# Two products instead of three in the feature-major GEMMs of a bidirectional SSD layer, with a new division of PSUM

## The chip, the core and the metric

The kernel runs on one core of one Trainium2 chip. The metric is the device time in microseconds of one execution, as a median of several. The data are float32; products are made in `float32r` on operands that are split into a high and a low part, so that the result has nearly float32 precision.

## What is computed

One layer on 256 tokens of 2048 features: a bidirectional Mamba-2 mixer (SSD), a cross-attention with 4 heads into 256 memory tokens, and a gated FFN with a convolution, each ahead of a residual add, and a last RMSNorm. Cut to what matters:

```python
u = rmsnorm(h, mix_norm)
z, xbc, dt_raw = split(u @ w_in)                       # 4096, 4096 + 2*8*128, 128
xs, B, C = split(silu(dwconv(xbc, conv_w, conv_b)))    # 64 heads of 64; 8 groups of state 128
y = ssd_scan(xs, dt_f, A_f, B, C) + flip(ssd_scan(flip(xs), ...)) + xs * d_skip
h = h + rmsnorm(y * silu(z), norm_g) @ w_out           # chunks of 128 tokens inside ssd_scan
u, mem_n = rmsnorm(h, xattn_norm), rmsnorm(mem, mem_norm)
q, (k, v) = u @ wq, split(mem_n @ wkv)
h = h + softmax(q k^T * 512**-0.5) v @ wo
gate, val = split(rmsnorm(h, ffn_norm) @ w_up)         # 5632 each
h = h + (silu(dwconv(gate)) * val) @ w_down
out = rmsnorm(h, final_norm)
```

## The kernel before

**Operands in two parts.** An activation operand is held in units (`new_unit`, line 94) of four feature tiles of 128 by 256 tokens, high and low part side by side, from a pool of 11. Weights come by DMA on SyncE's queue into `raw` (five buffers, line 115) in pieces of 1024 columns' worth per partition. ScalarE casts a piece to `w_hi` (line 106) and VectorE makes `w_lo` (line 107), four buffers each: 618 pieces in all.

**Three kinds of GEMM.** `gemm_feat` (line 132) puts features on the partitions and makes, for each of the contraction's tiles and each tile of 128 features, three products of 256 columns: high times high, high times low, low times high (lines 152 to 154). A PSUM tile of two banks takes four feature tiles. `gemm_feat_wide` (line 157) makes two: the high part of the weights meets both parts of the operand in one product of 512 columns (line 169), and the low part meets the high part in one of 256 (line 171). A feature tile then has a bank to itself, whose halves ScalarE (line 173) and VectorE (line 174) add up. Only the FFN's up-projection uses it. `gemm_tok` (line 176), for the values and the down-projection, puts tokens on the partitions.

**PSUM.** Eight banks: `ps_g`, two tiles of two banks for GEMMs by feature, and `ps_m`, four of one bank for all else (lines 60 and 61). Both are open from the first to the last instruction.

**Stages.** x is transposed and split; dt, its running sums and decays are made (to line 352). Then eight groups: `project(g+1)` (xs: four feature tiles, B and C: two; convolution and silu), `project_z(g)` (four), and `scan_group(g)` (line 389). The scan transposes xs and B, makes the two states that leave the chunks (line 415), and then for each of two chunks: a DMA broadcasts the running sums into `r` (line 420, one buffer), eight heads pass through ScalarE and VectorE (lines 431 and 432), an exponential (434), eight more passes (437 and 438), a product with it (440), TensorE's products with the incoming state (444) and with xs (449), and the additions (452 to 456). Behind the last group, `inv_rms` (line 223, matmuls 225 and 226, first reader 215) makes 1/rms of y in `r_ssd` (last instruction: line 221). Then come the memory tokens (a pool `memp` of their own, DMA in line 497, transposes in 515), w_out with the residual (`residual_units`, lines 476 and 484), queries, keys, values and attention, wo, and the FFN.

**What sets the order.** The Tile scheduler writes each engine's order: among the instructions that are ready in its own simulation it takes the one that is earliest in the program. It also sets the waits between pools that use the same memory one after the other.

Of the kernel before, what the change touches and what calls it, by code (L numbers as in the profile page):

```python
# [14 lines left out]
P = 128  # L15
T = 256
# [20 lines left out]
def kernel(  # L37
# [22 lines left out]
    ps_g = ctx.enter_context(tc.tile_pool(name="ps_g", bufs=2, space=bass.MemoryType.PSUM))  # L60
    ps_m = ctx.enter_context(tc.tile_pool(name="ps_m", bufs=4, space=bass.MemoryType.PSUM))
# [23 lines left out]
    # tri[:, 0, l] = 1 where l >= m, tri[:, 1, l] = 1 where l <= m  # L85
# [46 lines left out]
    def gemm_feat(units, wv, cols, k_first=0, first_raw=None):  # L132
        """features on the partitions: banks of two 128-feature tiles by 256 tokens"""
# [23 lines left out]
    def gemm_feat_wide(units, wv, c0, dst):  # L157
        """dst [P, 2, T] = two 128-feature tiles; the high part of the weights meets both parts of the
        operand in one product, so each tile has a bank whose halves add up to it"""
        nk = 4 * len(units)  # L160
        ps = psum_g()
        for k0 in range(0, nk, 4):
            hi, lo = load_weights(wv, k0, [(c0, 2 * P)])
            for kk in range(4):
                kt = k0 + kk
                unit = units[kt // 4]
                for ft in range(2):
                    fs = slice(ft * P, (ft + 1) * P)
                    nc.tensor.matmul(ps[:, ft, :], hi[:, kk, fs], unit[2][:, kt % 4].rearrange("p s t -> p (s t)"),  # L169
                                     start=(kt == 0), stop=False, skip_group_check=True)  # L170
                    nc.tensor.matmul(ps[:, ft, :T], lo[:, kk, fs], unit[0][:, kt % 4, :], start=False,  # L171
                                     stop=(kt == nk - 1), skip_group_check=True)
        nc.scalar.copy(out=dst, in_=ps[:, :, T:])
# [27 lines left out]
    def add_square(pool, acc, src2, first):  # L201
        """src2: [P, 2, T]"""
# [7 lines left out]
    def rsqrt_mean(pool, dst, total, n, tags=("rs_v", "rs_s")):  # L210
        """dst = (total / n + eps) ** -0.5: a square root from the table, then one Heron step"""
# [16 lines left out]

    r_mix = sb(const, [P, T], "r_mix")
# [7 lines left out]
    w_in_v = kview(w_in)  # L237
    units_mix = [new_unit() for _ in range(4)]
    with tc.tile_pool(name="xin", bufs=1) as xin:
# [9 lines left out]
        for u in range(4):  # L249
            stage = sb(xin, [P, 4, T], "x_stage", bufs=2)  # L250
            for jj in range(2):
                ps = psum_m()
# [19 lines left out]
        # the column of 1/rms as a row on every partition  # L272
# [12 lines left out]
    with tc.tile_pool(name="ssd", bufs=1) as ssd:  # L285
        acc_y = sb(ssd, [P, 2, T], "acc_y")

# [10 lines left out]
        # log1p(ex) = ln(w) * ex / (w - 1) with w = 1 + ex, and ex itself where w == 1  # L298
# [32 lines left out]
        # decay to the end of the chunk times dt: forward for chunk 0, backward for chunk 1  # L331
# [12 lines left out]
        # exp(cum) where a state comes in: forward rows in chunk 1, backward rows in chunk 0  # L344
# [9 lines left out]
        def conv_silu(banks, f0s, dst):  # L354
            """centred conv of 4 taps over the tokens, bias, silu; two feature tiles per bank"""
            for b, bank in enumerate(banks):
                s = sb(ssd, [P, 2, T], "cv_s", bufs=2)
                nc.vector.tensor_tensor(out=s, in0=two(bank), in1=rows2(r_mix), op=ALU.mult)
                a = dst[:, 2 * b:2 * b + 2, :]
                for j in range(2):  # L360
                    f = f0s[2 * b + j]
                    w = lambda t: pcol("conv_w", f * 4 + t)
                    nc.scalar.activation(out=a[:, j, :], in_=s[:, j, :], func=AF.Identity, scale=w(2), bias=pcol("conv_b", f))
                    for tap, off in ((0, 2), (1, 1)):
                        nc.vector.scalar_tensor_tensor(out=a[:, j, off:], in0=s[:, j, :T - off], scalar=w(tap),
                                                       in1=a[:, j, off:], op0=ALU.mult, op1=ALU.add)
                    nc.vector.scalar_tensor_tensor(out=a[:, j, :T - 1], in0=s[:, j, 1:], scalar=w(3),
                                                   in1=a[:, j, :T - 1], op0=ALU.mult, op1=ALU.add)
                nc.scalar.activation(out=a, in_=a, func=AF.Silu)

        def project(g):
            xs = sb(ssd, [P, 4, T], "xs", bufs=2)
            conv_silu(gemm_feat(units_mix, w_in_v, [(INNER + g * 512, 512)]), [g * 4 + j for j in range(4)], xs)
            bc = sb(ssd, [P, 2, T], "bc", bufs=2)
            conv_silu(gemm_feat(units_mix, w_in_v, [(2 * INNER + g * P, P), (2 * INNER + 1024 + g * P, P)]),
# [3 lines left out]
        def project_z(g):  # L379
            sz = sb(ssd, [P, 4, T], "sz")  # L380
            for b, bank in enumerate(gemm_feat(units_mix, w_in_v, [(g * 512, 512)])):
                nc.vector.tensor_tensor(out=sz[:, 2 * b:2 * b + 2, :], in0=two(bank), in1=rows2(r_mix), op=ALU.mult)
                nc.scalar.activation(out=sz[:, 2 * b:2 * b + 2, :], in_=sz[:, 2 * b:2 * b + 2, :], func=AF.Silu)
# [5 lines left out]
        def scan_group(g, xs, bc, sz):  # L389
            hs = slice(g * 8, (g + 1) * 8)  # L390
            er = sb(ssd, [P, 2, 4, P], "er")
            for q in range(2):
                for d in range(2):
                    nc.sync.dma_start(out=er[q * 64:(q + 1) * 64, d], in_=ecum_v[g, q, d].partition_broadcast(64))
            # token-major x and B
            xs_tok = sb(ssd, [P, 2, 512], "xs_tok")
            xsd = sb(ssd, [P, 2, 512], "xsd")
            for c in range(2):
                ps = psum_m()
                for j in range(4):  # L400
                    nc.tensor.transpose(out=ps[:, j * P:(j + 1) * P], in_=xs[:, j, c * P:(c + 1) * P], identity=ident)  # L401
                nc.scalar.copy(out=xs_tok[:, c, :], in_=ps)
                nc.vector.tensor_tensor(out=xsd[:, c, :].rearrange("p (h f) -> p h f", f=64),
                                        in0=ps.rearrange("p (h f) -> p h f", f=64),
                                        in1=dx_tok[:, c, hs].unsqueeze(2).broadcast_to([P, 8, 64]), op=ALU.mult)
            b_tok = sb(ssd, [P, 2, P], "b_tok")
            ps = psum_m()
            for c in range(2):
                nc.tensor.transpose(out=ps[:, c * P:(c + 1) * P], in_=bc[:, 0, c * P:(c + 1) * P], identity=ident)
            nc.scalar.copy(out=b_tok.rearrange("p c n -> p (c n)"), in_=ps[:, :T])  # L410
            # state that leaves chunk 0 forwards, and the one that leaves chunk 1 backwards
            st = sb(ssd, [P, 2, 512], "st")
            for c in range(2):
                ps = psum_m()
                nc.tensor.matmul(ps, b_tok[:, c, :], xsd[:, c, :], start=True, stop=True)  # L415
                nc.scalar.copy(out=st[:, c, :], in_=ps)
            for c in range(2):
                cl = slice(c * P, (c + 1) * P)
                r = sb(ssd, [P, 2, 8, P], "r")
                nc.sync.dma_start(out=r, in_=cum_v[c, g].partition_broadcast(P))  # L420
                ps_cb = psum_m()
                nc.tensor.matmul(ps_cb[:, :P], bc[:, 0, cl], bc[:, 1, cl], start=True, stop=True)
                cb = sb(ssd, [P, 2, P], "cb")
                nc.vector.tensor_tensor(out=cb, in0=ps_cb[:, :P].unsqueeze(1).broadcast_to([P, 2, P]), in1=tri, op=ALU.mult)  # L424

                # of the two exponents the one of the direction that reaches l from m is <= 0, the other >= 0
# [8 lines left out]
                for h in range(8):  # L435
                    hf, hb = g * 8 + h, 64 + g * 8 + h
                    nc.scalar.activation(out=t2[:, h, :], in_=cb[:, 1, :], func=AF.Copy, scale=dt_tok[:, c, hb:hb + 1])  # L437
                    nc.vector.scalar_tensor_tensor(out=t2[:, h, :], in0=cb[:, 0, :], scalar=dt_tok[:, c, hf:hf + 1],  # L438
                                                   in1=t2[:, h, :], op0=ALU.mult, op1=ALU.add)
                nc.vector.tensor_tensor(out=t2, in0=t2, in1=t1, op=ALU.mult)  # L440
                # what the incoming state gives, before its decay
                ps_o = psum_m()
                for j in range(4):
                    nc.tensor.matmul(ps_o[:, j * P:(j + 1) * P], st[:, 1 - c, j * P:(j + 1) * P], bc[:, 1, cl],  # L444
                                     start=(j == 0), stop=(j == 3), skip_group_check=True)
                ps_y = psum_m()
# [310 lines left out]
```

## Time and profile before

| | us |
|---|---|
| median of 3 runs (1871.98 to 1872.21) | 1872.16 |
| span of the profiled execution | 1870.4 |
| busy in that span: TensorE | 1851.4 |
| busy in that span: VectorE | 1246.3 |
| busy in that span: ScalarE | 1007.2 |

The span runs from the first to the last instruction. The page gives no time for the profiled execution but its span; 1.8 us of the median lie around it, if that execution was like the three. Matmuls are pipelined and their ends are modelled, so the distance from one start to the next tells what a product costs, and not its duration. "Idle before, releaser" tells how long an engine waited ahead of a group of instructions and what ended that.

### The profile page before, as it was taken

The page shows a single profiled execution, that of the slowest core. Times are in us where ns is not written, and L with a number is a line of the kernel's source. Part 1 is how long each engine was busy: PE and PEld are TensorE (multiplying, and loading weights), DVE is VectorE, ACT ScalarE, POOL GpSimd, SP SyncE. Part 2 cuts the span into 40 slices and gives each one's busy share as a digit, 9 for nine tenths or more (in the row PEclk, how much of TensorE's full clock was granted, in tenths as well). Part 3 has the DMA queues.
Part 4 walks back from the last instruction along what each step waited for, and adds up shares of the span by engine and source line. Part 5 has one row for each costly group of instructions (what it writes and reads, how often), then busy time and mean ns, then how long its engine had stood idle before and what let it go on. Part 6 is the DMA issues. An engine that isn't in the chain of part 4 may idle for free.

```text
span 1870.4 us, 31851 instructions
## 1 busy us (share of the span) xinstructions
PE 1851.4 (99%) x12845; PEld 1715.6 (92%) x12845; DVE 1246.3 (67%) x1764; ACT 1007.2 (54%) x1434; POOL 2.3 (0%) x11
## 2 busy tenths in 40 slices
PE   8999999999999999999999999999999999999997
PEld 8999999999999999999999998888888888888886
DVE  7778878988887756554454557666664556666654
ACT  6666767766675544444444446555553345555443
POOL 0000000000000000000000000000000000000000
PEclk9999999999999999999999999999999999999999
DMA  8667666766756655555555556566655565656553
GB/s 288 197 201 214 205 197 195 220 199 183 224 183 223 230 188 181 181 161 178 171 178 172 165 182 202 180 189 188 189 191 194 195 192 185 189 184 189 188 195 113
DMA packets 256947, 359.06 MB, mean 192 GB/s; under 512 B 11616, under 2 KB 145120, under 8 KB 256288
## 3 DMA queue, kind: packets, MB, share of 16 engines
q1 hardware_dynamic: 256720, 356.76, 60.8%
q8 instruction: 100, 1.64, 0.4%
q14 instruction: 47, 0.39, 0.1%
q0 software_dynamic: 80, 0.28, 0.0%
HBM read 352.60 MB, written 4.39 MB: 191 GB/s over the span
## 4 chain that ended last, share of the span: by engine, by line
PE 99%; DMA 0%; DVE 0%; ACT 0%; SPq 0%; issue 0%; DVEq 0%
PE psg L169 18%; PE psg L154 17%; PE psg L152 16%; PE psg L153 16%; PE psg L171 9%; PE psm L190 6%; PE psm L191 6%; PE psm L189 6%; PE psm L449 1%; PE psm L444 1%; PE psm L415 1%; PE psm L572 0%; PE psm L570 0%; PE psm L571 0%; DMA x<-in_x_dram 0%; PE psm L401 0%
## 5 line engine op out<-in xcount | busy, mean ns | idle before, releaser
L107 DVE TENSOR_TENSOR w_lo<-raw,w_hi 128x1024 fp32r<-128x1024 f32 x618 | 753.4, 1223 | 518.4 <-ACT w_hi L106 515.7
L106 ACT CAST w_hi<-raw 128x1024 fp32r<-128x1024 f32 x618 | 645.1, 1048 | 697.7 <-PE psg L153 255.0
L154 PE MATMUL psg<-unit,w_lo 128*128 128x256 f32 x2576 | 733.4, 285 | 0.0
L152 PE MATMUL psg<-unit,w_hi 128*128 128x256 f32 x2576 | 731.6, 284 | 0.0
L153 PE MATMUL psg<-unit,w_hi 128*128 128x256 f32 x2576 | 730.3, 284 | 0.0
L154 PEld LDWEIGHTS psg<-unit,w_lo 128*128 128x128 f32 x2576 | 494.3, 192 | 3.4 <-issue 3.1
L152 PEld LDWEIGHTS psg<-unit,w_hi 128*128 128x128 f32 x2576 | 494.4, 192 | 1.7 <-issue 1.7
L153 PEld LDWEIGHTS psg<-unit,w_hi 128*128 128x128 f32 x2576 | 494.5, 192 | 0.3 <-issue 0.2
L169 PE MATMUL psg<-unit,w_hi 128*128 128x512 f32 x1408 | 493.5, 396 | 0.0
L171 PE MATMUL psg<-unit,w_lo 128*128 128x256 f32 x1408 | 393.2, 279 | 0.0
L169 PEld LDWEIGHTS psg<-unit,w_hi 128*128 128x128 f32 x1408 | 264.3, 188 | 63.6
L171 PEld LDWEIGHTS psg<-unit,w_lo 128*128 128x128 f32 x1408 | 265.2, 188 | 0.1
L189 PE MATMUL psm<-w_hi,unit 128*128 128x512 f32 x480 | 186.8, 389 | 0.0
L190 PE MATMUL psm<-w_lo,unit 128*128 128x512 f32 x480 | 186.8, 389 | 0.0
L191 PE MATMUL psm<-w_hi,unit 128*128 128x512 f32 x480 | 186.8, 389 | 0.0
L189 PEld LDWEIGHTS psm<-w_hi,unit 128*128 128x128 f32 x480 | 90.1, 188 | 18.8
L190 PEld LDWEIGHTS psm<-w_lo,unit 128*128 128x128 f32 x480 | 90.1, 188 | 18.6
L191 PEld LDWEIGHTS psm<-w_hi,unit 128*128 128x128 f32 x480 | 90.1, 188 | 18.5
L431 ACT ACTIVATE r<-r,ncum_tok 128x128 f32<-128x128 f32 x128 | 39.4, 390 | 57.7 <-DMA r<-cum_d 55.1
L432 DVE SCALAR_TENSOR_TENSOR r<-r,ncum_tok 128x128 f32<-128x128 f32 x128 | 36.9, 347 | 17.1 <-ACT r L431 17.1
L437 ACT ACTIVATE t<-cb,dt_tok 128x128 f32<-128x128 f32 x128 | 39.1, 388 | 0.7 <-DVE cb L424 0.2
L438 DVE SCALAR_TENSOR_TENSOR t<-cb,dt_tok,t 128x128 f32<-128x128 f32 x128 | 36.5, 348 | 3.3 <-ACT t L437 3.3
(218 smaller groups left out, 1044.7 us busy)
## 6 DMA issues: line engine op xcount, KB each, us to landing
raw<-in_w_up_dram SPq DMA_DIRECT2D x176, 512.0 KB, 3.6
raw<-in_w_in_dram SPq DMA_DIRECT2D x130, 512.0 KB, 4.6
raw<-in_w_down_dram SPq DMA_DIRECT2D x88, 512.0 KB, 3.6
raw<-in_w_out_dram SPq DMA_DIRECT2D x64, 512.0 KB, 4.3
raw<-in_wkv_dram SPq DMA_DIRECT2D x64, 512.0 KB, 3.7
raw<-in_w_in_dram SPq DMA_DIRECT2D x64, 256.0 KB, 4.5
r<-cum_d SPq DMA_DIRECT2D x16, 1024.0 KB, 6.3
raw<-in_wq_dram SPq DMA_DIRECT2D x32, 512.0 KB, 3.6
```

Source lines behind the costliest of these rows:

```text
L106: nc.scalar.copy(out=hi, in_=src)
L107: nc.vector.tensor_tensor(out=lo, in0=src, in1=hi.bitcast(F32), op=ALU.subtract)
L152: nc.tensor.matmul(dst, wh, uh, start=first, stop=False, skip_group_check=True)
L153: nc.tensor.matmul(dst, wh, ul, start=False, stop=False, skip_group_check=True)
L154: nc.tensor.matmul(dst, wl, uh, start=False, stop=last, skip_group_check=True)
L169: nc.tensor.matmul(ps[:, ft, :], hi[:, kk, fs], unit[2][:, kt % 4].rearrange("p s t -> p (s t)"), start=(kt == 0), stop=False, skip_group_ ...
L171: nc.tensor.matmul(ps[:, ft, :T], lo[:, kk, fs], unit[0][:, kt % 4, :], start=False, stop=(kt == nk - 1), skip_group_check=True)
L189: nc.tensor.matmul(banks[tt], uh, hi[:, kk, :], start=(kt == 0), stop=False)
L190: nc.tensor.matmul(banks[tt], uh, lo[:, kk, :], start=False, stop=False)
L191: nc.tensor.matmul(banks[tt], ul, hi[:, kk, :], start=False, stop=(kt == nk - 1))
L431: nc.scalar.activation(out=t1[:, h, :], in_=t1[:, h, :], func=AF.Identity, bias=ncum_tok[:, c, hf:hf + 1])
L437: nc.scalar.activation(out=t2[:, h, :], in_=cb[:, 1, :], func=AF.Copy, scale=dt_tok[:, c, hb:hb + 1])
```

## The change

- `gemm_feat_wide` takes a list of columns and returns its PSUM tile; adding up the halves is now `add_halves`. xs, B and C, z, w_out, queries, keys and wo all use it, 256 features at a time. `gemm_feat` stays for dt alone (16 steps of the contraction).
- Up to the end of the scan, `inv_rms` of y included, PSUM is one pool of four tiles of two banks; it is then closed and `ps_g` (2) and `ps_m` (4) are opened in its place.
- The scan's transposes, states, masks `cb`, the products with the incoming state and their decay, and the last additions are done for both chunks in one instruction each; `ps_o` comes ahead of the chunks' loop and `ps_y` is held through both.
- The memory tokens' norm and transposes stand behind w_out in the program, in tiles of the attention's pool.

```diff
-    ps_g = ctx.enter_context(tc.tile_pool(name="ps_g", bufs=2, space=bass.MemoryType.PSUM))
-    ps_m = ctx.enter_context(tc.tile_pool(name="ps_m", bufs=4, space=bass.MemoryType.PSUM))
+    psum = {}
+    def psum_pools(scope, **bufs):
+        psum.clear()
+        for name, n in bufs.items():
+            psum[name] = scope.enter_context(tc.tile_pool(name="ps_" + name, bufs=n, space=bass.MemoryType.PSUM))
     def psum_g():
-        return sb(ps_g, [P, 2, 512], "psg")
+        return sb(psum["g"], [P, 2, 512], "psg")
     def psum_m():
-        return sb(ps_m, [P, 512], "psm")
+        return sb(psum["m"], [P, 512], "psm") if "m" in psum else psum_g()[:, 0, :]
...
+    def add_halves(dst, ps):
         nc.scalar.copy(out=dst, in_=ps[:, :, T:])
         nc.vector.tensor_tensor(out=dst, in0=ps[:, :, :T], in1=dst, op=ALU.add)
...
+    ssd_psum = ctx.enter_context(ExitStack())
+    psum_pools(ssd_psum, g=4)
...
-        def conv_silu(banks, f0s, dst):
-            for b, bank in enumerate(banks):
-                s = sb(ssd, [P, 2, T], "cv_s", bufs=2)
-                nc.vector.tensor_tensor(out=s, in0=two(bank), in1=rows2(r_mix), op=ALU.mult)
+        def conv_silu(ps, f0s, a):
+            s = sb(ssd, [P, 2, T], "cv_s", bufs=2)
+            add_halves(s, ps)
+            nc.vector.tensor_tensor(out=s, in0=s, in1=rows2(r_mix), op=ALU.mult)
...
+            for b in range(2):
+                conv_silu(gemm_feat_wide(units_mix, w_in_v, [(INNER + g * 512 + b * 256, 256)]),
+                          [g * 4 + 2 * b, g * 4 + 2 * b + 1], xs[:, 2 * b:2 * b + 2, :])
...
+            ps = psum_g()
+            for c in range(2):
+                nc.tensor.matmul(ps[:, c, :], b_tok[:, c, :], xsd[:, c, :], start=True, stop=True)
+            nc.scalar.copy(out=st, in_=ps)
+            ps_o = psum_g()
+            for c in range(2):
+                for j in range(4):
+                    nc.tensor.matmul(ps_o[:, c, j * P:(j + 1) * P], st[:, 1 - c, j * P:(j + 1) * P],
+                                     bc[:, 1, c * P:(c + 1) * P], start=(j == 0), stop=(j == 3), skip_group_check=True)
+            nc.vector.tensor_tensor(out=er, in0=ps_o.rearrange("p c (j l) -> p c j l", l=P), in1=er, op=ALU.mult)
+            ps_y = psum_g()
             for c in range(2):
...
+            for j in range(4):
+                xj = xs[:, j, :].rearrange("p (c l) -> p c l", l=P)
+                nc.vector.scalar_tensor_tensor(out=xj, in0=xj, scalar=pcol("dskip", g * 4 + j),
+                                               in1=ps_y[:, :, j * P:(j + 1) * P], op0=ALU.mult, op1=ALU.add)
+            xv = xs.rearrange("p j (c l) -> p c j l", l=P)
+            nc.vector.tensor_tensor(out=xv, in0=xv, in1=er, op=ALU.add)
...
         inv_rms(ssd, acc_y, r_ssd, INNER, ("cb", "b_tok"))
+    ssd_psum.close()
+    psum_pools(ctx, g=2, m=4)
-    def residual_units(pool, hT, banks, u, gname, acc_t, r=None):
+    def residual_units(pool, hT, units, wv, u, gname, acc_t, r=None):
...
+        for b in range(2):
+            ps = gemm_feat_wide(units, wv, [(u * 512 + b * 256, 256)])
             hv = hT[:, u * 4 + 2 * b:u * 4 + 2 * b + 2, :]
             if r is None:
-                nc.vector.tensor_tensor(out=hv, in0=two(bank), in1=hv, op=ALU.add)
+                nc.vector.tensor_tensor(out=hv, in0=ps[:, :, T:], in1=hv, op=ALU.add)
+                nc.vector.tensor_tensor(out=hv, in0=ps[:, :, :T], in1=hv, op=ALU.add)
             else:
                 t = sb(pool, [P, 2, T], "res_t", bufs=2)
-                nc.vector.tensor_tensor(out=t, in0=two(bank), in1=rows2(r), op=ALU.mult)
+                add_halves(t, ps)
+                nc.vector.tensor_tensor(out=t, in0=t, in1=rows2(r), op=ALU.mult)
                 nc.vector.tensor_tensor(out=hv, in0=t, in1=hv, op=ALU.add)
...
+            def split_wide(dst, units, wv, c0):
+                for b in range(2):
+                    t = sb(att, [P, 2, T], "res_t", bufs=2)
+                    add_halves(t, gemm_feat_wide(units, wv, [(c0 + b * 256, 256)]))
+                    split_plain(dst[0][:, 2 * b:2 * b + 2, :], dst[1][:, 2 * b:2 * b + 2, :], t)
+                return dst
```

## Rows read from the trace of the kernel before

**Rows 1.** The page: span, busy time by engine, the chain that ended last by engine.
```profile
span 1870.4 us, 31851 instructions
PE 1851.4 (99%) x12845; PEld 1715.6 (92%) x12845; DVE 1246.3 (67%) x1764; ACT 1007.2 (54%) x1434; POOL 2.3 (0%) x11
PE 99%; DMA 0%; DVE 0%; ACT 0%; SPq 0%; issue 0%; DVEq 0%
```
**Rows 2.** Waits of TensorE, past its start: us in total, times, longest.
```profile
PE psm L449 <- DVE t L440: 1.4, 1, 1.4
```
**Rows 3.** Groups by line: count, busy us, mean ns of one, idle before.
```profile
L152 PE MATMUL psg<-unit,w_hi 128*128 128x256 f32 x2576 | 731.6, 284 | 0.0
L169 PE MATMUL psg<-unit,w_hi 128*128 128x512 f32 x1408 | 493.5, 396 | 0.0
L174 DVE TENSOR_TENSOR f_s<-psg,f_s 128x512 f32<-128x512 f32 x44 | 30.1, 684 | 0.0
L173 ACT COPY f_s<-psg 128x512 f32<-128x512 f32 x44 | 25.6, 582 | 0.6 <-DVE r_ffn L221 0.6
```
**Rows 4.** A window in w_out, line 154 alone: window, length, PE busy (count).
```profile
640.00:740.00 100.00, 78.64 (x278) 53.30 (x279) 1.00 0.57 189
```
**Rows 5.** Two windows of the up-projection: line 169 alone, columns as in rows 4.
```profile
1180.00:1380.00 200.00, 200.00 (x578) 108.16 (x578) 1.00 0.61 190
1540.00:1740.00 200.00, 200.00 (x568) 106.37 (x567) 1.00 0.60 186
```
**Rows 6.** Windows, all lines: length; PE, PEld, DVE, ACT, POOL busy; clock; DMA. A group.
```profile
180.00:245.00 65.00, 65.00 (x549) 63.43 (x548) 55.06 (x101) 44.98 (x78) 0.00 (x0) 1.00 0.66 203
```
**Rows 7.** Waits of ScalarE and VectorE in that group, 180 to 245 us.
```profile
ACT w_hi L106 <- PE psg L153: 6.7, 5, 1.8
DVE w_lo L107 <- ACT w_hi L106: 4.5, 5, 1.6
```
**Rows 8.** Waits of SyncE's queue at the first DMA into a newly opened pool.
```profile
SPq L635 <- DVE r_ffn L221: 1.6, 1, 1.6
SPq L497 <- DVE r_ssd L221: 1.3, 1, 1.3
```
**Rows 9.** Timeline around that DMA, VectorE and SyncE: start, length.
```profile
590.18 0.42 DVE L215 TENSOR_SCALAR cb<-psm 128x256 f32<-128x256 f32 x1
597.11 1.75 DVE L221 RECIPROCAL r_ssd<-cb 128x256 f32<-128x256 f32 x1
598.93 0.82 SPq L497 DMA_DIRECT2D mem<-in_mem_dram  x2
```
**Rows 10.** Timeline of the last scan: first transposes, eight activations, the products of line 440.
```profile
536.42 1.10 PE L401 MATMUL psm<-ident,xs 128*128 128x128 f32 x8
557.84 1.22 DVE L440 TENSOR_TENSOR t<-t,r 128x1024 f32<-128x1024 f32 x1
566.69 2.45 ACT L431 ACTIVATE r<-r,ncum_tok 128x128 f32<-128x128 f32 x8 [5.69 <-DMA r<-cum_d]
574.82 1.23 DVE L440 TENSOR_TENSOR t<-t,r 128x1024 f32<-128x1024 f32 x1 [1.15 <-ACT r L434]
```
**Rows 11.** Window over that scan and `inv_rms`: psg alone (TensorE first), w_lo alone (VectorE third), all.
```profile
536.40:590.60 54.20, 46.02 (x368) 44.69 (x369) 1.28 (x2) 0.00 (x0) 1.00 0.60 193
...
536.40:590.60 54.20, 34.87 (x123) 23.56 (x123) 18.35 (x16) 1.00 0.60 193
...
536.40:590.60 54.20, 52.79 (x440) 50.85 (x439) 46.45 (x90) 38.77 (x71) 0.00 (x0) 1.00 0.60 193
```
**Rows 12.** The broadcasts into r of that group: from issue to landing.
```profile
DMA to landing us min/median/max: 7.3/7.4/7.5
```
**Rows 13.** The window at the span's end (columns as in rows 6); timeline at its start.
```profile
1862.00:1870.00 8.00, 0.00 (x0) 0.00 (x0) 3.20 (x8) 1.33 (x2) 0.00 (x0) 0.50 0.70 263
...
13.75 0.41 PE L154 MATMUL psg<-unit,w_lo 128*128 128x256 f32 x1
13.97 0.41 PE L152 MATMUL psg<-unit,w_hi 128*128 128x256 f32 x1
```

More of the change, by code (lines that the diff above doesn't have):

```diff
@@ L380, in project_z @@
             sz = sb(ssd, [P, 4, T], "sz")
-            for b, bank in enumerate(gemm_feat(units_mix, w_in_v, [(g * 512, 512)])):
-                nc.vector.tensor_tensor(out=sz[:, 2 * b:2 * b + 2, :], in0=two(bank), in1=rows2(r_mix), op=ALU.mult)
-                nc.scalar.activation(out=sz[:, 2 * b:2 * b + 2, :], in_=sz[:, 2 * b:2 * b + 2, :], func=AF.Silu)
+            for b in range(2):
+                z = sz[:, 2 * b:2 * b + 2, :]
+                add_halves(z, gemm_feat_wide(units_mix, w_in_v, [(g * 512 + b * 256, 256)]))
+                nc.vector.tensor_tensor(out=z, in0=z, in1=rows2(r_mix), op=ALU.mult)
+                nc.scalar.activation(out=z, in_=z, func=AF.Silu)
             return sz
@@ L400, in scan_group @@
                 for j in range(4):
[L401 to L405, printed above, removed]
+                    nc.tensor.transpose(out=ps[:, c, j * P:(j + 1) * P], in_=xs[:, j, c * P:(c + 1) * P], identity=ident)
@@ L410, in scan_group @@
[L410 to L416, printed above, removed]
+                nc.tensor.transpose(out=ps[:, 0, c * P:(c + 1) * P], in_=bc[:, 0, c * P:(c + 1) * P], identity=ident)
             for c in range(2):
                 cl = slice(c * P, (c + 1) * P)
+                nc.tensor.matmul(ps[:, 1, cl], bc[:, 0, cl], bc[:, 1, cl], start=(c == 0), stop=(c == 1), skip_group_check=True)
@@ new lines, in scan_group @@
+            nc.scalar.copy(out=st, in_=ps)
+            ps_o = psum_g()
+            for c in range(2):
+                for j in range(4):
[3 more added lines that the diff above has]
+            ps_y = psum_g()
@@ L419, in scan_group @@
+            for c in range(2):
                 r = sb(ssd, [P, 2, 8, P], "r")
                 nc.sync.dma_start(out=r, in_=cum_v[c, g].partition_broadcast(P))
[L421 to L424, printed above, removed]
                 t1 = r[:, 0]
@@ L439, in scan_group @@
                                                    in1=t2[:, h, :], op0=ALU.mult, op1=ALU.add)
                 nc.vector.tensor_tensor(out=t2, in0=t2, in1=t1, op=ALU.mult)
[L442 to L446, printed above, removed]
                 for h in range(8):
-                    dst = ps_y[(h % 2) * 64:(h % 2 + 1) * 64, (h // 2) * P:(h // 2 + 1) * P]
+                    dst = ps_y[(h % 2) * 64:(h % 2 + 1) * 64, c, (h // 2) * P:(h // 2 + 1) * P]
@@ L449, in scan_group @@
                     nc.tensor.matmul(dst, xs_tok[:, c, h * 64:(h + 1) * 64], t2[:, h, :],
                                      start=(h < 2), stop=(h >= 6), skip_group_check=True)
-                for j in range(4):
-                    nc.vector.scalar_tensor_tensor(out=xs[:, j, cl], in0=xs[:, j, cl], scalar=pcol("dskip", g * 4 + j),
-                                                   in1=ps_y[:, j * P:(j + 1) * P], op0=ALU.mult, op1=ALU.add)
-                yo = er[:, 1 - c]
-                nc.vector.tensor_tensor(out=yo, in0=ps_o.rearrange("p (j l) -> p j l", l=P), in1=yo, op=ALU.mult)
@@ L456, in scan_group @@
-                nc.vector.tensor_tensor(out=xs[:, :, cl], in0=xs[:, :, cl], in1=yo, op=ALU.add)
+            for j in range(4):
[4 more added lines that the diff above has]
+            nc.vector.tensor_tensor(out=xv, in0=xv, in1=er, op=ALU.add)
@@ L659, in ffn_unit @@
                     s = sb(ffn, [P, 2, T], "f_s", bufs=2)
[L660 removed]
+                    add_halves(s, gemm_feat_wide(units_ffn, w_up_v, [(FFN + i * 512 + b * 256, 256)]))
                     nc.vector.tensor_tensor(out=s, in0=s, in1=rows2(r_ffn), op=ALU.mult)
```

123 lines of the change are left out of this document (64 added, 59 removed).

## The prediction

> **What bounds the kernel now.** I read the page's busy shares and its chain first: TensorE is busy for 1851.4 of 1870.4 us, and the chain that ended last is TensorE for 99% [rows 1]. The waits of TensorE come next, because a busy engine could still be waiting at the ends of its matmuls: past the first transposes of x it waits once in the whole span, 1.4 us at the last scan [rows 2]. So time is won only by giving TensorE fewer or shorter products, and anything new that TensorE has to wait for is added at its full length. For the price of a product I took windows of a steady stretch with one line alone, and counted: the distance between starts, not the modelled duration. Last I read the one place where the change touches the order: the end of the scan.
>
> **Part 1: three products become two.** Line 152 ran 2576 times [rows 3]; 16 of these are dt's and stay, so 2560 sets of three become a pair. A set of three: 278 in 100 us in w_out, 0.3597 us [rows 4]. A pair, in the FFN, which has it already: 578 in 200 us, 0.3460 us, in one stretch, and 568, 0.3521 us, in a later one, with the same code [rows 5]. I found no cause for the two speeds, so I keep both ends: 2560 x 0.0137 = 35.1 us, 2560 x 0.0076 = 19.5 us. The FFN has both for about equally long, so I take the middle, **27.3 us less**. Columns are the same either way (768 a set); what goes is one weight load and one start of a product.
>
> By the Trainium skill (TensorE: Matmul & The Clock Gate, Back-to-back issue gap) a product at full clock follows the last one after N/2.4 + 2.5 ns, and the next weights load under it. An estimate from that formula is 327.5 ns for three and 324.7 ns for the pair, so some 7 us in all in place of 27. The rows disagree: the set of three takes 359.7 ns and the pair 346.0 or 352.1.
>
> **Part 2: the drains.** Each pair of feature tiles now needs a copy on ScalarE and an addition on VectorE (0.582 and 0.684 us [rows 3]): 40 tiles in the SSD stage, 24 in w_out, queries and keys, and 8 additions more in wo. Over the span VectorE is busy for 67% [rows 1], and the SSD stage lies above that mean, so attention, w_out and wo lie below it; there the drains lie beside products, and a PSUM tile has the 11 us or more of the next GEMM (32 pairs) to be emptied. Nothing. In the SSD stage cover is thin: in a group of 65.0 us VectorE is busy for 55.1 [rows 6]. Five additions bring 3.4 us, against about 1 us saved by merging, and the group shrinks to 65.0 - 160 x 0.0107 = 63.3 us: 57.5 of 63.3. Against that, its idle time is mostly slack: what it waits for is ScalarE's cast, and ScalarE waits for TensorE to free a weight buffer, 6.7 us in a group [rows 7], so weights lie ready ahead of TensorE. Bounds: nothing; or, if none of VectorE's idle time can shrink, 65.0 + 2.4 - 63.3 = 4.1 us in each of 8 groups, 33 us. I take 3 us in all, near the lower end because of rows 7. The two-bank tiles should not stall it: a scan holds two at a time, a GEMM one, and one is being emptied.
>
> **Part 3: PSUM is closed and opened again.** This is the step that I expect to decide. How a pool waits for the one whose memory it takes over is seen in SBUF: the first DMA into `memp` waits on SyncE's queue for line 221 [rows 8], the last instruction that reads a tile of the scan's pool, and goes at 598.93, just behind its end at 598.86 [rows 9]; the DMA of `fn_bc` into the FFN's pool waits for the last reader in attention's pool in the same way [rows 8]. Before, no PSUM pool was closed, so no row shows it for PSUM; I expect the same. Then the first product of w_out waits until line 215, the last reader of the scan's PSUM (590.18 + 0.42 = 590.60 [rows 9]), is done. Behind it on TensorE stands everything that is left; ScalarE and VectorE can cast four pieces ahead and SyncE can load five, and then these wait too.
>
> What that costs: before, the last z ends and the last scan's transposes start at 536.42 [rows 10]. Until 590.60 are 54.2 us, in which TensorE made 368 products of w_out [rows 11], 368 x 0.12 = 44.1 us; 10.1 us were the scan's own products and waits. After, none of the 368 can be there, and the stretch is as long as scan and `inv_rms` take alone. VectorE, busy for 46.5 of those 54.2 us, spent 18.4 on weights [rows 11]; with these gone 35.9 are left, and merging the chunks' last additions puts chunk 0's share behind chunk 1, some 1.5 us: 37.4. Less the 10.1 that were there anyway: **27.3 us more**. Lower bound, from what can't be shortened: one broadcast of 7.4 us [rows 12] (the first may lie ahead of 536.42), for each chunk eight activations of 2.45 us together and the product of 1.23, and the 14.5 us from that product's end at 576.05 [rows 10] to 590.60, less weights by their share of the stretch, 18.4 / 54.2: 7.4 + 7.4 + 9.6 = 24.4, so 14 more. Upper bound: nothing is gained, 54.2 - 10.1 = 44. I take the middle one, as VectorE's time for weights is what is known to fall away.
>
> Clock: in the window behind the last products the granted clock is 0.50 (1.2 GHz), and at the start the products begin 0.21 us apart and not 0.12 [rows 13]. In the gap there are only short bursts, so those, and the first microseconds of w_out, may run at the lower level: between 0 and 4 us, I take **2**.
>
> **Part 4: moved and merged steps.** The memory tokens are read only by the first keys, behind w_out and a query. Their DMAs (four of 512 KB for two of 1 MB), 32 transposes and 32 splits pass w_out's weight loads on SyncE and lie beside w_out's products as they did: nothing; with that cover gone, it would be the 3 us of transposes. The load of the residual no longer waits for `memp`. 1/rms of y comes 8.3 us behind line 215 [rows 9], and w_out's first PSUM tile isn't full for 64 x 0.349 = 22 us. Merged scan instructions take no product from TensorE.
>
> **Sum.** 1872.2 - 27.3 + 3 + 27.3 + 2 = **1877 us**. It is made on the profiled span, 1870.4, and moved to the median by the 1.8 us around it.
>
> **Rivals.**
> 1. *No gap at the scan's end*: a PSUM bank is passed on when its own last reader is done, or products of w_out get ahead. For it: nothing shows PSUM behaving like SBUF. Against: rows 8. Then 1872.2 - 27.3 + 3 = 1848 us, 1840 to 1856: faster. It decides from the point where the gap is under 18 us.
> 2. *VectorE becomes the bound of the SSD stage*: 57.5 of 63.3 us leaves little room for instructions in a fixed order. TensorE would wait for `w_lo` in each group. 1877 + 30 = 1907. Against: rows 7.
> 3. *The third weight load was hidden all along*: with no gain from the pair, 1877 + 27 = 1904. Rows 4 and 5 speak against it, and it needs the scan to behave otherwise than the FFN. The skill's formula above would make it 1897.
>
> **How the numbers follow.** A change of 0.2% (3.7 us) is about what a measurement can tell from none; so "same" is 1868.4 to 1875.9. The forecast with a gap has 0.72: 0.34 slower, 0.22 same, 0.16 faster, since a short gap with the quick pair (1856) is faster. Its own range is 1862 to 1896: parts 1 and 3 are independent, so their distances to the ends (7.8 and 13 below, 7.8 and 17 above) add as squares. Rival 1 has 0.14 (faster), rival 2 0.10 and rival 3 0.04 (slower). Faster 0.30, same 0.22, slower 0.48. Both signs are likely, so beside that range stands the one of all cases, 1850 to 1897: half of rival 1 is left out below (0.07), and above it rivals 2 and 3 for the most part.
>
> **What would show it.** Right: windows of the SSD stage, w_out, queries, keys and wo with pairs 0.346 to 0.352 us apart; no wait of TensorE of over 1 us per group; then, from the last z on, one stretch of some 35 us without any psg product but the scan's, a wait of TensorE that line 215 ends, and a lower granted clock in it. Wrong: w_out's products between the last scan's steps (rival 1), waits of TensorE for `w_lo` in every group (rival 2), or pairs 0.36 us apart (rival 3).

## The result, and the profile after

| | median, us | runs | ratio to before, 95% interval |
|---|---|---|---|
| before, run beside it | 1872.07 | 1870.69 to 1872.21 (4) | |
| after | 1978.87 | 1978.06 to 1986.29 (4) | 1.0581, 1.0563 to 1.0598 |

The change makes the kernel 107 us slower. The prediction was 1877 us with a range of 1850 to 1897; the result is 82 us above that range's end.

The page of after: span, busy time, TensorE's busy share and granted clock in 40 slices, and the chain that ended last.

```profile
span 1976.3 us, 26766 instructions
PE 1869.0 (95%) x10285; PEld 1606.8 (81%) x10285; DVE 1293.5 (65%) x1774; ACT 1040.4 (53%) x1479; POOL 2.3 (0%) x11
PE   5999899889888799999999999999999999999997
PEclk7999999999997899999999999999999999999999
PE 92%; ACT 4%; DVE 3%; DMA 1%; issue 0%; SPq 0%; DVEq 0%; ACTq 0%
```

Beside [rows 1] three things differ. TensorE has 2560 products fewer, as meant, and yet a longer busy time. Its share is below nine tenths in slices of the first 14, which reach to the end of the scan, least in the first and the 14th, and in the last slice, as in before; in the first, the 13th and the 14th the granted clock is lower too. And ScalarE and VectorE now hold 7% of the chain.

Where the time lies can be read from five starts that both programs have: the first transposes of xs in the first and in the last scan, and the first product of each of the three `inv_rms` (y, the residual behind w_out, the residual behind wo).

| us | start to first scan | first to last scan | last scan to `inv_rms` of y | to that of w_out | to that of wo | to the end |
|---|---|---|---|---|---|---|
| before | 114.9 | 421.5 | 52.7 | 155.0 | 388.7 | 737.6 |
| after | 142.2 | 475.3 | 36.6 | 195.6 | 385.7 | 740.9 |

Of 106 us, 27 are lost ahead of the first scan, 54 in the groups and 24 around the end of the scan (the last scan is 16 us shorter and w_out 41 longer, as no product of w_out is left in that scan). Behind w_out nothing is lost, but nothing is gained either: the 768 sets of queries, keys and wo should save 6 to 11 us by part 1, and against them stand the moved memory tokens (4.8 us by themselves, below) and 3.3 us in the FFN, whose code is the same.

The waits of TensorE in after, largest first (us in total, times, longest). In before it had one of 1.4 us past its start [rows 2].

```profile
PE psg L445 <- ACT st L440: 32.4, 8, 4.8
PE psg L439 <- DVE xsd L420: 18.2, 7, 2.6
PE psg L335 <- DVE r L325: 12.5, 1, 12.5
PE psg L234 <- DVE acc_y L217: 7.5, 1, 7.5
PE psg L269 <- DMA x<-in_x_dram: 6.3, 5, 4.6
PE psg L469 <- DVE t L466: 4.2, 1, 4.2
PE psg L439 <- ACT b_tok L431: 3.4, 1, 3.4
```

Lines 439, 445 and 469 are the scan's own steps (states, incoming state, y); 439 and 445 wait once in each of the 8 groups for the step ahead of them. No wait is for `w_lo` or for a drain. These are waits within the scan's chain; what is new is that nothing fills them. The timeline of TensorE through one scan of after, from the last z product ahead of it to the first GEMM product behind it (start, length, line, count, idle time before):

```profile
142.06 0.28 PE L176 MATMUL psg<-unit,w_lo 128*128 128x256 f32 x1
142.17 1.03 PE L418 MATMUL psg<-ident,xs 128*128 128x128 f32 x8
143.04 0.38 PE L427 MATMUL psg<-ident,bc 128*128 128x128 f32 x2
143.26 0.61 PE L430 MATMUL psg<-bc 128*128 128x128 f32 x4
146.48 1.96 PE L439 MATMUL psg<-xsd,b_tok 128*128 128x512 f32 x4 [2.60 <-DVE xsd L420]
153.21 3.79 PE L445 MATMUL psg<-bc,st 128*128 128x128 f32 x16 [4.77 <-ACT st L440]
156.92 1.98 PE L469 MATMUL psg<-t,xs_tok 128*64 128x128 f32 x16
158.83 0.52 PE L174 MATMUL psg<-unit,w_hi 128*128 128x512 f32 x1
```

For 16.7 us there is no GEMM product. The first 16.6 us of the first scan in both kernels: for before all work on `psg`, which only GEMMs use there (window, length, busy time and count of TensorE, weight loads, VectorE, ScalarE and GpSimd, then the granted clock), and for after the pair's first product alone (line 174; columns of [rows 4]).

```profile
114.90:131.50 16.60, 13.10 (x99) 11.93 (x97) 1.29 (x2) 0.00 (x0) 1.00 0.50 144
```

```profile
142.20:158.80 16.60, 0.02 (x1) 0.00 (x0) 0.80 0.44 128
```

99 products against one. The granted clock over it is 0.80 and not 1.00: a part of the stretch ran at 1.2 GHz. All engines in two whole groups of after, beside the 65.0 us of [rows 6], and in the stretch from the last z product to the first of w_out:

```profile
142.20:216.60 74.40, 67.02 (x389) 57.25 (x387) 57.12 (x97) 47.80 (x81) 0.00 (x0) 0.95 0.62 177
216.60:288.80 72.20, 66.24 (x388) 56.63 (x387) 57.65 (x98) 47.57 (x81) 0.00 (x0) 0.95 0.62 182
...
623.20:656.60 33.40, 14.70 (x69) 10.14 (x66) 22.48 (x47) 19.63 (x41) 0.00 (x0) 0.60 0.22 76
```

VectorE does 57 us of work in a group as forecast (57.5), and has room in the 72 to 74. The first product of w_out, behind the gap, and what it waited for:

```profile
656.62 0.79 PE L174 MATMUL psg<-unit,w_hi 128*128 128x512 f32 x1 [0.52 <-DVE cb L224]
```

Line 224 is the first reader in `inv_rms`, which is line 215 in before: the wait that part 3 forecast.

### The profile page after: what moved, and what is told of

It is laid out like the page before. It is cut to its first block, busy times and chain, and to the rows that moved or that the text cites. A ratio compares the mean times of both kernels' runs of the same rounds, so it can differ in the third digit from the quotient of the medians.

```text
span 1976.3 us, 26766 instructions
## 1 busy us (share of the span) xinstructions
PE 1869.0 (95%) x10285; PEld 1606.8 (81%) x10285; DVE 1293.5 (65%) x1774; ACT 1040.4 (53%) x1479; POOL 2.3 (0%) x11
## 4 chain that ended last, share of the span: by engine, by line
PE 92%; ACT 4%; DVE 3%; DMA 1%; issue 0%; SPq 0%; DVEq 0%; ACTq 0%
PE psg L174 47%; PE psg L176 24%; PE psm L199 6%; PE psm L198 6%; PE psm L200 6%; ACT t L463 2%; PE psg L445 1%; PE psg L469 1%; ACT w_hi L111 1%; DVE w_lo L112 1%; DVE xsd L420 0%; PE psm L605 0%; PE psm L604 0%; PE psm L603 0%; DMA raw<-in_w_in_dram 0%; ACT st L440 0%
## 5 line engine op out<-in xcount | busy, mean ns | idle before, releaser
L174 PE MATMUL psg<-unit,w_hi 128*128 128x512 f32 x3968 | 1397.0, 397 | 1.8 <-DVE unit L107 1.3
L174 PEld LDWEIGHTS psg<-unit,w_hi 128*128 128x128 f32 x3968 | 746.7, 188 | 177.6 <-issue 2.3
L445 PEld LDWEIGHTS psg<-bc,st 128*128 128x128 f32 x128 | 27.2, 323 | 40.8 <-ACT st L440 40.8
L445 PE MATMUL psg<-bc,st 128*128 128x128 f32 x128 | 29.2, 420 | 32.4 <-ACT st L440 32.4
L439 PE MATMUL psg<-xsd,b_tok 128*128 128x512 f32 x32 | 21.7, 816 | 21.6 <-DVE xsd L420 18.2
L439 PEld LDWEIGHTS psg<-xsd,b_tok 128*128 128x128 f32 x32 | 7.4, 256 | 29.0 <-issue 25.4
L183 DVE TENSOR_TENSOR f_s<-psg,f_s 128x512 f32<-128x512 f32 x44 | 30.1, 684 | 0.0
L377 DVE SCALAR_TENSOR_TENSOR xs<-cv_s,par,xs 128x254 f32<-128x254 f32 (+1 forms) x64 | 27.7, 483 | 0.0
```

Of the source, the lines that this page charges most:

```text
L445: nc.tensor.matmul(ps_o[:, c, j * P:(j + 1) * P], st[:, 1 - c, j * P:(j + 1) * P], bc[:, 1, c * P:(c + 1) * P], start=(j == 0), stop=(j == ...
```

## The experiments

After the result I had three theories. **S**: the scan's tiles and the GEMMs' tiles now come out of one pool, the scan asks first, and so the next GEMM has no PSUM tile until the scan lets go of one. **D**: the added drains load ScalarE and VectorE, and the scan's steps come late for that. **M**: merging the chunks has made the scan's chain longer. All runs do the whole computation; the runs of before beside them had medians of 1871.7 to 1872.0 us. A time without a range or a ratio is that of a single run.

### The two products alone

Before, with the pair in every GEMM; PSUM, scan and memory tokens as they were.

```diff
-            conv_silu(gemm_feat(units_mix, w_in_v, [(INNER + g * 512, 512)]), ...)
+            for b in range(2):
+                conv_silu(gemm_feat_wide(units_mix, w_in_v, [(INNER + g * 512 + b * 256, 256)]), ...)
...                                    (the same in z, w_out, queries, keys and wo)
```

> The kernel before with two products instead of three and nothing else: its PSUM pools (two tiles of two banks, four of one bank, never closed), its scan and its place of the memory tokens stay. Theory S (in the changed kernel the scan's tiles take the shared PSUM slots ahead of the next GEMM's tile, so TensorE has no products between the scan's steps): the group stays below its 65.0 us, and the time is 1872 less 20 to 35 us, 1837 to 1852. Theory D (the drains overload ScalarE and VectorE in the SSD stage): the group grows to about 73 us as in the changed kernel, 1920 or more. Theory M (merging the two chunks in the scan lengthens its chain): as S, since the scan is the old one.

Measured: 1896.1 us, ratio 1.0137 (1.0120 to 1.0154). A miss of 44 us. From the first to the last scan it took 421.2 us, as before and not longer, which speaks against D's 73 us a group. S had expected less, and TensorE is busy for only 413.6 of them: some 8 us that the pair saved went into waits for drains (line 177 is VectorE's addition), five for xs, B and C and one of 2.8 us for a z. And w_out took 181.8 us in place of 155.0. The longest wait of TensorE stands in it, at 606 us:

```profile
PE psg L168 <- DVE cv_s L177: 4.8, 5, 1.2
PE psm L506 <- ACT junk L492: 11.2, 1, 11.2
```

Line 506 is the transposes of the memory tokens, which wait for their norm. They stood there in before too, and cost nothing: the two PSUM tiles of w_out held four feature tiles each, 32 steps x 4 tiles x 0.36 us = 46 us of products each and 92 us in all. A tile of the pair's form holds two, 32 x 2 x 0.35 = 22 us, so 44 us in all, and then TensorE reached the transposes before their data. That is a cost of the pair which the prediction had not seen: *halving what a PSUM tile holds halves the work that lies ready on TensorE.*

### Closing and reopening alone

Before, with its two pools closed behind `inv_rms` of y and opened again with the same sizes.

```diff
         inv_rms(ssd, acc_y, r_ssd, INNER, ("cb", "b_tok"))
+    ssd_psum.close()
+    psum_pools(ctx, g=2, m=4)
```

> The kernel before with its two PSUM pools closed behind the last 1/rms of y and opened again with the same sizes; nothing else. In the changed kernel the stretch from the last z to the end of w_out is 18.8 us longer than before, and w_out's own products are some 3 us shorter, so closing should cost about 22 us: 1894, with a wait of TensorE on line 215 and no w_out product before it. If a bank is passed on as soon as its own reader is done: 1872. Theories S, D and M expect groups of 65.0 us alike.

Measured: 1879.2 us, 7 us more than before. TensorE's and VectorE's rows at the point where the products of w_out begin, and at `inv_rms` (line 232):

```profile
544.22 1.27 DVE L389 TENSOR_TENSOR sz<-psg,r_mix 128x512 f32<-128x512 f32 x2
545.54 0.58 PE L159 MATMUL psg<-unit,w_hi 128*128 128x256 f32 x1 [0.54 <-DVE sz L389]
...
584.13 0.59 PE L232 MATMUL psm<-acc_y,ones 128*128 128x256 f32 x2
```

Between the two, GEMM products alone (TensorE busy and count first):

```profile
545.50:584.10 38.60, 35.51 (x272) 35.12 (x272) 0.00 (x0) 0.00 (x0) 0.93 0.46 154
```

The first product of w_out runs 39 us ahead of `inv_rms`, although the pools are closed behind that in the program. What it waits for is line 389, the drain of the last z, which is the last reader in the GEMMs' old pool. So a tile of the new `ps_g` doesn't wait for the readers in the other pool that was closed with it (`inv_rms` used `ps_m`). Whether it waits for the readers of its own banks or for the last one in its whole old pool, this run can't tell: both are line 389. The price is the time from the last scan's first transposes to that drain, 10.1 us in which TensorE was busy for 5.1.

### Two pools of two

After, with two of the four two-bank tiles for GEMMs and two for everything else up to the scan's end; order, drains, merged scan and closing are those of after.

```diff
-    psum_pools(ssd_psum, g=4)
+    psum_pools(ssd_psum, g=2, s=2)
...                                    (scan, transposes of x and dt: psum_s() in place of psum_g())
```

> The changed kernel, but up to the scan's end GEMMs by feature have two tiles of two banks of their own, and all else (the scan, dt, the transposes of x) two tiles of two banks of its own; still closed at the scan's end. Theory S: the first wide product starts at about 32 us and not 51, and groups come down from 73 to 64 us or less; the gap at the end and the memory tokens stay: 1978 less 20 to 27 less 7 x 9.5, 1885 to 1892. Theory M: groups stay at some 73 us, 1950 or more. Theory D: the same, 1950 or more.

Measured: 1874.8 us, 104 us less than after. First scan at 116.6 us, first to last scan 419.5, the next two 52.4 and 158.1. Two groups, the two behind them, and the longest wait:

```profile
155.40:283.10 127.70, 127.37 (x774) 109.67 (x773) 112.74 (x196) 93.43 (x161) 0.00 (x0) 1.00 0.69 206
283.10:413.60 130.50, 128.68 (x773) 110.87 (x772) 114.00 (x196) 94.05 (x162) 0.00 (x0) 0.99 0.69 201
```

```profile
PE pss L440 <- ACT unit L107: 7.8, 1, 7.8
```

TensorE is busy for 127.4 of 127.7 us with the same drains and the same merged scan, at full clock; in the two groups behind them it waits 1.8 us for a drain. So a group takes 64 to 65 us. D and M, which wanted 1950 us or more, are out; S had expected 10 us more than came, since it still counted a gap for closing.

### One pool alone

Before, three products and old scan, with the one pool of four up to the scan's end, closed there as in after.

```diff
-    ps_g = ctx.enter_context(tc.tile_pool(name="ps_g", bufs=2, ...))     # two banks
-    ps_m = ctx.enter_context(tc.tile_pool(name="ps_m", bufs=4, ...))     # one bank
+    psum_pools(ssd_psum, g=4)
```

> The kernel before with its three products and its old scan, one chunk at a time, but with PSUM as in the changed kernel: one pool of four tiles of two banks up to the scan's end, then closed and opened as two and four. Theory S: groups of 70 us or more, a late first product, and the gap: 1872 + 22 + 7 x 6 to 10 + 20 to 27, 1955 to 1990. Theory M: groups of 65 us, 1894. Theory D: groups of 65 us, 1894.

Measured: 2065.5 us: 194 us more than before and 75 above S's range, without a new pair, a new drain or a merged scan. A group, and the wait that leads:

```profile
226.90:311.80 84.90, 70.46 (x548) 67.98 (x547) 56.92 (x101) 45.57 (x78) 0.00 (x0) 0.88 0.53 155
```

```profile
PE psg L457 <- DVE t L448: 95.8, 16, 8.8
```

Line 457 is the scan's y, once for each chunk. The old scan asks for eleven tiles in a group (two for the transposes of xs, one for those of B, and two each for states, masks, incoming state and y) and the merged one for five; a group takes 84.9 us with eleven and 73.3 with five. Of the 11.6 us between them some 2 are the pair's; the rest I put down to the six requests that merging saves. That is argued from these two kernels; merging by itself wasn't run.

### The memory tokens alone

Before, with the memory tokens' stage moved behind w_out.

```diff
+            inv_rms(att, acc_h, r_xa, D)
+            units_mem = [new_unit() for _ in range(4)]   # norm and transposes, from ahead of w_out
```

> The kernel before with one edit: the norm and the transposes of the memory tokens are issued behind the output projection of the scan, as in the kernel after. Prediction: nothing, 3 us if their cover is gone. The trace of after shows TensorE waiting there three times, 1.5 to 2.0 us each, 5 to 6 us in all. Theory S (the loss is in the PSUM tiles): 1875 to 1880 us. Rival, the move is hidden in three-product code since its GEMM banks last longer: 1871 to 1874 us.

Measured: 1876.8 us, 4.8 more and as S expected, from one run beside thirteen of before (1870.5 to 1873.9). The wait:

```profile
PE psm L530 <- DVE v_hi L522: 3.8, 1, 3.8
```

### The two products and the memory tokens

The first experiment with that one edit more.

> Two products in every GEMM by feature, the PSUM pools of before never closed, the scan of before, and the memory tokens behind the output projection: the run of the two products alone with that one thing more. Theory R (the run of two products alone was slow because its first two output tiles, 2 feature tiles each instead of 4, were full after some 44 us and had to wait for the memory tokens, whose PSUM they need): the output projection goes back from 182 us to 155 to 160 us and the time is 1862 to 1876 us. Rival, the wide tiles are short of room whatever stands behind the scan: 1890 to 1897 us as in that run.

Measured: 1882.7 us, ratio 1.0056 (1.0039 to 1.0073). w_out goes from 181.8 to 159.5 us as expected, so the stall there was the memory tokens; the total misses by 7 us. What is left is the last scan, where TensorE waits 6.2 us for `b_tok` and 3.7 us for a drain, and the groups, where it waits for drains as in the first run: 4.1 us once for a z, and 4.9 us in five waits.

### The GEMMs' pool never closed

The two pools of two, where only the other one is closed and opened again.

```diff
-    psum_pools(ssd_psum, g=2, s=2)
+    psum_pools(ctx, g=2)
+    psum_pools(ssd_psum, s=2)
```

> The kernel of the split pools (after, with two of the four two-bank tiles for GEMMs alone and two for all else up to the scan's end) with one edit: the pool of the GEMMs is never closed, only the other is closed behind the scan and opened again. Theory S: the 8 us in which TensorE stood in the last scan go, since the output projection can start under it: 1862 to 1868 us. Rival, that gap is the chain of the last scan itself and stays: 1873 to 1876 us.

Measured: 1872.2 us (1868.0 to 1875.7, ten runs), ratio 1.0001 (0.9992 to 1.0010), so the rival was nearer. TensorE still stands 7.6 us at the states of the last scan. With a pool of its own for the GEMMs, closing it or not makes no difference that these runs show.

### The same pool, another order

After, pool of four, closing and start untouched; in the program the scan's five tiles and the GEMMs' five of a group are asked for in turn.

```diff
-            nxt = project(g + 1); sz = project_z(g); scan_group(g, *cur, sz)
+            gemms = chain(project(g + 1, nxt), project_z(g, szs))     # a step is one PSUM tile
+            scan = scan_group(g, *cur, szs)
+            for _ in range(5):
+                next(scan)
+                next(gemms, None)
```

> The kernel after with one edit: in the program the scan's five PSUM tiles and the GEMMs' five tiles of a group stand in turn (transposes, x, B, x, states, B and C, out, z, y, z) instead of the five GEMM tiles first and the scan's five behind them. Pool, number of tiles, closing and start are those of after. Theory S in its sharper form (slots go out in the order in which the program asks for them, so five scan tiles in a row keep the next GEMM out): the groups go back from 73 to some 65 us, 50 to 60 us less than after, 1918 to 1930 us; the 27 us of the start and the 19 us at the end stay. Rival, four two-bank tiles are too few for both whatever the order: 1960 us or more.

Measured: 1894.3 us, 85 us less than after and 24 less than expected. A group (all engines), the three long waits that are left, and that of w_out's first product:

```profile
275.40:338.20 62.80, 62.80 (x388) 54.66 (x386) 55.98 (x98) 49.20 (x83) 0.00 (x0) 1.00 0.68 205
```

```profile
PE psg L336 <- DVE r L326: 12.2, 1, 12.2
PE psg L235 <- DVE acc_y L218: 7.4, 1, 7.4
PE psg L477 <- DVE t L474: 5.0, 1, 5.0
PE psg L175 <- DVE cb L225: 0.5, 1, 0.5
```

All groups take 62.8 or 62.9 us, some 2.2 less than in before, and TensorE never waits in them. Four two-bank tiles are enough; the order in which they are asked for decides. What stays is outside the groups: the dt chain (line 336), and the last scan and `inv_rms` (lines 477 and 235), where no GEMM stands between. From the last scan to `inv_rms` of w_out it takes 28.7 us more than before, and the first product of w_out still waits for `inv_rms` (the fourth row, line 225): the gap of part 3 is still there.

### Own pools and this order

Both edits: two pools of two, the GEMMs' never closed, tiles asked for in turn.

> Two edits of the runs before together: the split pools of which the GEMMs' is never closed (run at 1872.2 us), and the program in which scan tiles and GEMM tiles stand in turn. Theory S: the 8 us in which TensorE stood at the states of the last scan are covered by the z product of that group, which now stands behind the scan's first steps: 1860 to 1867 us, faster than before. Rival, the gap only moves to another step of the last scan: 1870 to 1875 us.

Measured: 1858.0 us (1856.6 to 1863.4, five runs), ratio 0.9929 (0.9915 to 0.9943): faster than before, by 14 us, and 2 below S's range. Its trace is that of the slowest of the five, 1863.4 us. From within the last scan into w_out, all engines:

```profile
530.00:580.00 50.00, 50.00 (x304) 42.62 (x303) 40.03 (x56) 29.78 (x43) 0.00 (x0) 1.00 0.60 195
```

### The start

The one pool with tiles asked for in turn, with the GEMM tiles of group 0 asked for ahead of the dt chain's.

> The run in which scan tiles and GEMM tiles stand in turn in the one pool of four (1894.3 us), with one more edit: the three GEMM tiles of group 0 are asked for ahead of the PSUM tiles of the dt chain instead of behind them. Theory S: TensorE no longer stands through the dt chain (12.2 us at one wait, 27 us later at the first scan): 1866 to 1876 us. Rival, the start is slow because the drains and the clock are, not because of the order of the requests: 1888 us or more.

Measured: 1886.1 us, 8 us less than with that order alone, where 18 to 28 were expected. The wait of 12.2 us is gone, and the first scan starts at 76.0 us in place of 86.8. But the dt chain's own steps now start at 64.0 us, behind the three GEMM tiles, and TensorE stands some 8 us in them. So the order is part of the 27 us that after loses at its start; own pools bring back nearly all (first scan at 116.6 us, 114.9 in before).

## Why the prediction was wrong

**The step that failed** is one sentence at the end of part 2: "The two-bank tiles should not stall it: a scan holds two at a time, a GEMM one, and one is being emptied." It counted tiles that are held. What decides is the order in which they are asked for: in the program the scan's five stand between z and the next group's x, so the products that used to fill the scan's waits have no tile. The part put this at nothing; it cost 16.7 us without a GEMM product in each scan, groups of 73.3 us where it had 63.3, and 54 us from the first to the last scan. The run with own pools (same order) and the run with the same pool (other order) each bring the groups back, to 64 to 65 and 62.8 us; the one pool alone, without the pair, the drains and the merged scan, costs 194 us. The slot itself isn't in the trace; that it is a matter of slots follows from these three runs together.

It could have been priced roughly from before, by the GEMM products between the steps of a scan, counted as part 3 counted the 368 of the last one [rows 11]: 99 in its first 16.6 us, 99 x 0.12 = 11.9 us in a group. (The 16.6 us are read from after; before shows the count for any length.) Changing the order gave back 10.5 us in each whole group.

The gap that returns with each group is what the Trainium skill (Perfetto Trace Analysis, Optimization Strategy) calls consistent bubbles, a sign that there may be too little SBUF or PSUM for the next tile, by count or size of buffers. The trace agrees in the sign; the run with the same count and size in another order shows that neither need be at fault.

**Point by point.**

- *Part 1, the pair (27.3 us less, 19.5 to 35.1).* Right, where nothing waits. In the run with the same pool in another order, 160 sets save 2.2 us, 13.8 ns each, the upper end (13.7). In the profiled execution of the fastest run the first product of `inv_rms` behind wo comes 16.0 us earlier than in before; with the memory tokens' 4.8 these are 20.8 us for 2560 sets, 8.1 ns each, near the lower end (7.6), and w_out runs at the slower speed there. The FFN, whose code is the same, is 7.3 us longer in it, at the slower speed in both halves. Rival 3, no gain, is out. The formula beside the rows gives 325.0 ns for the pair and not 324.7, so 6.4 us and not 7; no term rests on it.
- *Part 2, the drains (3 us).* About right, and not what made after slow: none of its waits is for a drain, and in the run with another order TensorE is busy for 62.80 of 62.80 us with all of them. Where GEMMs have two tiles and the order is the old one, they do cost: 7.6 us in the groups of the first run, 3.7 and 4.6 us with two pools of two. Rival 2, a bound by VectorE, is out: no wait for `w_lo` stands among those of after, and the fastest run has six, 3.7 us in all. What the part left out is that a tile of two feature tiles instead of four halves the products that lie ready (27 us in w_out in the first run).
- *Part 3, closing PSUM (27.3 us more).* The gap came with the size and the signs that the part named: from the end of the last z product at 623.16 to w_out's first at 656.62 there are 33.5 us without a GEMM product, where the part had 37.4; the first one waits for the reader in `inv_rms`; and the two sections around it are 24.5 us longer. Whether closing is its cause stays open. Closing costs 7 us in before, where it lets 272 products of w_out run ahead of `inv_rms` as in rival 1, and nothing that can be seen beside own pools. In both cases the GEMMs' old pool holds no tile of the last scan. In after the one pool holds the last scan's tiles and that of `inv_rms`, and one pool that is never closed wasn't run. The rule that was read from [rows 8], a wait for the last reader of the whole old pool, fits after and the run with closing alone; a wait for the readers of the same banks isn't ruled out.
- *The clock (2 us, at the gap alone).* Too narrow. The granted clock is lower in more places than the gap: 0.80 in the first 16.6 us of the scans, and 0.60 in the gap.
- *Part 4, moved memory tokens (nothing, 3 if the cover is gone).* 4.8 us. The transposes were priced, not what they wait for: the norm (3.8 us in that run). *Merged scan: takes no product from TensorE.* Right: with it TensorE is busy for 62.80 of 62.80 us. In a shared pool it seems to help, by asking for fewer tiles.
- *What would show it.* "No wait of TensorE of over 1 us per group" was the sentence to fail first: two such waits stand in each, 2.6 and 4.8 us in the first.
- *The chances.* Slower had 0.48, and slower it is, mainly by a term that the sum doesn't have, which is luck: no rival said that the scan would lose its filling. All rivals were variations of the parts that had already been priced. The division of PSUM is in the change's title, and it got one sentence.

From after to the fastest run: 1978.9, less 84.6 for the order, less 36.3 for own pools of which the GEMMs' stays open, is 1858.0. Taken the other way round, own pools give 106.6 and the order 14.2.

## What to carry to other kernels

When a pool becomes common to a stream that must never stop and to a chain with waits, list the requests in program order and see which ones stand ahead of the stream's next tile: a count of what is held at one time doesn't tell. Keep the stream's tiles in a pool of their own, or ask for both kinds in turn; here either gave back 85 to 104 of 107 us, and both together turned the change into a gain of 0.7%. And where tiles hold less, recount how many microseconds of work lie ready on the engine, because what stood hidden behind it (here 11 us of waiting for a norm) comes out.

## What the runs showed of the hardware

**The pair's two speeds come with no change in its code.** Weight and operand tiles and loop are the same, and yet w_out runs at 290 pairs in 100 us in the run with the same pool in another order and at 284 in the next one (window over line 175: length, TensorE busy and count); the first half of the FFN's up-projection runs at 289 and at 284.

```profile
600.00:700.00 100.00, 100.00 (x290) 53.91 (x289) 1.00 0.61 196
```

```profile
600.00:700.00 100.00, 100.00 (x284) 53.18 (x283) 1.00 0.60 191
```

The clock is 1.00 in both. At 0.0073 us a pair this is 19 us over 2560 pairs; its cause stays open, and wasn't tried.

**Behind 10 us with waits the clock was at its lower level.** In the run with closing alone TensorE did the last scan's steps with waits from 535.4 us, and then the products of w_out began. Windows over that, then the first products, then the next ones (all engines, granted clock behind the five busy times):

```profile
535.40:545.50 10.10, 5.12 (x28) 3.41 (x24) 9.13 (x22) 6.97 (x20) 0.00 (x0) 0.93 0.90 266
545.50:550.80 5.30, 5.26 (x24) 5.26 (x25) 4.74 (x14) 5.27 (x13) 0.00 (x0) 0.50 0.07 14
550.80:555.50 4.70, 4.70 (x41) 4.67 (x39) 3.79 (x5) 2.96 (x4) 0.00 (x0) 1.00 0.15 49
```

24 products took 5.3 us at 0.50 (1.2 GHz), 0.22 us each; at 1.00 (2.4 GHz) it is 41 in 4.7 us, 0.115 each (products that overlap the window's ends are counted), or 0.12 from one start to the next. So behind the 10 us of a half idle engine these 24 products cost some 2.4 us more.
